# Values' high and low part side by side in one stationary operand, and the meta tokens' small products over 128 rows, in a two-layer hybrid trunk

## The chip, the cores and the metric

The kernel runs on one core of one Trainium2 chip. The metric is the device time of one execution in microseconds. The engines of a core are TensorE (PE in the rows; its weight loads PEld), VectorE (DVE), ScalarE (ACT), GpSimd (POOL) and SyncE (SP), which issues the transfers. TensorE multiplies a stationary operand, up to 128 rows by 128 columns, by a moving one, and adds into PSUM.

## The reference

The input is 512 frames of 1024 features. 16 learned meta tokens stand before them, so 528 positions count; the reference's pads are masked everywhere. There are two layers. Each normalises, multiplies by one wide in-projection, runs two mixers, multiplies each mixer's output by a SiLU gate, and multiplies the whole by an out-projection that is added to the stream.

```python
# layer AB
oa = dsa_attention(...)            # 8 heads of 64: top-k keys by an indexer, softmax, weights @ values
oa = oa.reshape(bsz, P, -1) * jax.nn.silu(ag)
log_a = jax.nn.log_sigmoid((ba @ gate_w2 + gate_b)) / GLA_TAU
ob = gla_chunked(...)              # 4 heads: keys of 64, values of 128, chunks of 64 positions
ob = head_rms(ob).reshape(bsz, P, -1) * jax.nn.silu(bg)
h = h + jnp.concatenate([oa, ob], axis=-1) @ w_out
# layer CD
oc = retention_chunked(...)        # 4 heads like GLA's, with fixed decay
od = stick_breaking(...)           # 8 heads of 64: w = exp(log_sigmoid(z) + after), w @ values
```

What the change touches is the product of a head's weights (queries by keys) with its values, in dsa_attention and stick_breaking, and what is computed for the 16 meta tokens as a chunk of their own in both recurrent mixers.

## The kernel before

Activations lie with features on the partitions and positions in the free dimension. Most products need more digits than TensorE's faster 32-bit type keeps, so operands are split into a high part (`hh`, `wh`, `vh`, `ph`) and a low part, the rest (`hl`, `wl`, `vl`, `pl`). A product of two such numbers is three matmuls: high by high, high by low and low by high. A weight tile `raw` arrives by DMA, ScalarE writes its high part `wh`, VectorE subtracts to get `wl`, and the projections accumulate in PSUM as `acc`.

The four attention pairs of layer AB (A0 to A3) and the four stick-breaking pairs of layer CD (S0 to S3) each treat two heads, the even one and the odd one (`odd`). `pair` (L1070) runs a string of steps: S computes scores and weights for a head, T transposes the weights to have keys on the partitions and splits them into `ph` and `pl` (`weights_turned`, L1039), M does the same for the meta keys (`weights_meta`, L1025, 96 rows that hold high, low and high part), and P (`weighted`, L1057) multiplies by values. The second digit, `u`, is the half of the queries: 256 frames each. The value tiles hold for each pair 192 columns: even head, 64 zeros, odd head (`values`, L966, `value_steps`, L998). `vcols` (L1021) cuts 128 of them, so that the even head's result lands in partitions 0 to 63 and the odd head's in 64 to 127 of one PSUM tile `y` of 512 columns. There is one buffer of y (`pv`). When the pair is done, VectorE multiplies y by the gates into `mx`.

Layer AB begins with the indexer: VectorE finds the top 128 scores of each row by repeated MAX and MATCH_REPLACE on the `lt` tiles. The two pairs of GLA heads (G0, G1) and the values run beside that. The heads of GLA and retention work with 64 rows of keys, and their meta chunk with 16 rows: `gla_steps` (L1331) makes `m`, with the meta keys by queries, their transpose `ktm` (a `mid` buffer), the masked products `attm`, and the products with the meta values `vm` (`head_values`, L1232). `finish_head` (L1392) transposes the 16-row `om`, `residual` (L1405) the 16-row `xm` of each 128-feature part of the input, and `index_weights` (L870) takes 64-row parts of `ba`.

The order of the work is not written out. A recorder keeps every operation (L167), and a planner (`order`, L286) then places them: each engine's next operation is the one that by its costs (`price`, L216) can start first, ties by due time. For TensorE a change of the row class between 32, 64 and 128 costs 95 ns in its plan (`ROWS`), and among operations that are late the ones of the same class are preferred. The program is issued from one line, L406, which is why all rows say L406.

The lines on which most rests:

```python
dst = o[:, P * b0:P * (b0 + nb)]
xh, xl = self.vcols(vh[j], p, odd), self.vcols(vl[j], p, odd)
nc.tensor.matmul(dst, xh, ph, start=False, stop=False)
nc.tensor.matmul(dst, xh, pl, start=False, stop=False)
nc.tensor.matmul(dst, xl, ph, start=False, stop=last and i == len(parts) - 1)
```

Of the kernel before, what the change touches and what calls it, by code (L numbers as in the profile page):

```python
# [9 lines left out]
F32 = mybir.dt.float32  # L10
# [6 lines left out]
P = 128  # L17
# [392 lines left out]
class Kernel:  # L410
# [48 lines left out]
    def vt(self, dt=F32):  # L459
        return self.wk.tile([P, 768], dt, tag="vt", bufs=8, name=self.name("vt"))  # L460
# [228 lines left out]
    def late_consts(self):  # L689
# [8 lines left out]
        self.w2 = self.cp.tile([P, 256], F32, name="w2")  # L698
        nc.sync.dma_start(self.w2[96:112, :], ins["gla_gate_w2"][0])
# [5 lines left out]
        self.attm = [self.cp.tile([NMETA, NMETA], F32, name=f"attm{i}") for i in range(2)]  # L705
        for t in self.attm:
            nc.gpsimd.memset(t, 0.0)
        self.ptm = self.cp.tile([96, 512], F32R, name="ptm")
# [142 lines left out]
    def indexer(self, first, a):  # L851
# [4 lines left out]
        nc.vector.tensor_copy(self.ba[64:128], a[64:128])  # L856
# [13 lines left out]
    def index_weights(self):  # L870
        tr = self.tr()
        for b in range(NB):
            self.transpose(tr[:, 64 * b:64 * b + 64], self.ba[64:128, blk(b)])
        self.nc.vector.tensor_copy(self.iw, tr[:, :256].rearrange("p (b c) -> p b c", b=NB)[:, :, 0:8])
        yield 1
# [90 lines left out]
    def values(self, src, col):  # L966
# [20 lines left out]
        for f in range(4):  # L987
# [7 lines left out]
            self.add(self.value_steps(f, v, vh, vl, vm), self.LAG["v"], f"v{f}")  # L995
        return vh, vl, vm

    def value_steps(self, f, v, vh, vl, vm):  # L998
# [14 lines left out]
        c = slice(P * f, P * (f + 1))  # L1013
        t = self.tr()
        self.transpose(t[:32, :P], z.rearrange("p o c -> p (o c)"))
        self.hi(vm[0:32, c], t[:32, :P])
        self.hi(vm[32:64, c], t[:32, :P])
        self.lo(vm[64:96, c], t[:32, :P], vm[0:32, c])
        yield 1

    def vcols(self, t, p, odd):  # L1021
        return t[:, 192 * p + 64 * odd:192 * p + 64 * odd + P]
# [46 lines left out]

    def pair(self, scores, pm, v, p, gates, tmp, lag, meta=None):  # L1070
# [4 lines left out]
        for word in self.PAIR.split():  # L1075
# [27 lines left out]
        self.nc.vector.tensor_tensor(tmp[:, NMETA:], o, gates[0][:, NMETA:], op=ALU.mult)  # L1103
# [49 lines left out]
    def attention_steps(self, p, qs, ks, kl, strips, gates):  # L1153
# [3 lines left out]
        lm = self.tiny([NMETA, 2, NMETA])  # L1157
# [648 lines left out]
```

## Time and profile before

| what | value |
|---|---|
| runs, median (lowest to highest) | 653.55 us (652.32 to 654.64), 3 runs |
| profiled execution, and its span | 654.6 us, 652.7 us |
| mean granted clock of TensorE | 0.986 of full speed |
| TensorE busy | 633.3 us, 97% of the span |
| VectorE busy | 483.5 us, 74% |
| ScalarE busy | 406.3 us, 62% |
| the chain of waits that ended last | TensorE 78%, VectorE 12%, ScalarE 8% |

The span runs from the first to the last instruction; 1.9 us of the execution lie around it. Names in a row are tiles: `y<-pt,vt` is a matmul that writes y from weights `pt` and values `vt`. A timeline row with a count covers that many instructions that follow each other, and since matmuls overlap, the time that one takes is read from the start of one row to the start of the next. A shape such as 16*128 is the tile of TensorE in use, rows by columns.

### The profile page before, as it was taken

Reading aid. Unit: us, or ns where it says so; the run is one execution under the profiler, and the core shown is the slowest. Engines: PE = TensorE matmul, PEld = TensorE weight load, DVE = VectorE, ACT = ScalarE, POOL = GpSimd, SP = SyncE. Lnnn points to the kernel's source line nnn. Section 1 sums busy time; section 2 is a strip of 40 time slices with the busy share of each in tenths; the row PEclk is TensorE's granted clock in tenths of the full one; section 3 lists DMA queues with packets and bytes.
Section 4 is the critical chain, followed back from the end, with each engine's and each line's share of the span. In section 5 each row is a group of like instructions: output and inputs, shape, how many; then the busy total and the mean of one; then the engine's idle time right before and its main releaser. Section 6 shows DMA issues by size and latency. Waiting matters only on the chain.

```text
span 652.7 us, 12208 instructions
## 1 busy us (share of the span) xinstructions
PE 633.3 (97%) x4469; PEld 582.8 (89%) x4469; DVE 483.5 (74%) x1182; ACT 406.3 (62%) x912; POOL 68.9 (11%) x116
## 2 busy tenths in 40 slices
PE   7999999899999999999999999999999999999995
PEld 6979999898989999999899999888998888988884
DVE  6768799899977859779642674699945699966643
ACT  5656563362344868599643675799844699944434
POOL 4000100120010000001122110001200001110030
PEclk9899999799999999999999999999999999999998
DMA  8437223232322323112243272203322203235403
GB/s 245 111 83 230 66 66 83 58 90 52 80 66 77 89 66 99 50 49 66 65 132 115 65 238 87 66 17 98 82 83 65 77 5 98 65 98 157 150 17 129
DMA packets 91103, 59.25 MB, mean 91 GB/s; under 512 B 7314, under 2 KB 81628, under 8 KB 91044
## 3 DMA queue, kind: packets, MB, share of 16 engines
q1 hardware_dynamic: 91044, 58.48, 31.4%
q8 instruction: 35, 0.57, 0.3%
q14 instruction: 24, 0.20, 0.1%
HBM read 53.18 MB, written 6.90 MB: 92 GB/s over the span
## 4 chain that ended last, share of the span: by engine, by line
PE 78%; DVE 12%; ACT 8%; issue 2%; POOL 0%; DVEq 0%; ACTq 0%; POOLq 0%
PE acc L406 53%; PE x L406 17%; PE y L406 8%; ACT wt L406 4%; DVE st L406 2%; DVE wt L406 2%; DVE wl L406 2%; DVE lt L406 1%; ACT st L406 1%; DVE pt L406 1%; DVE m L406 1%; ACT wh L406 1%; DVE kl L406 1%; ACT ptm L406 1%; ACT pt L406 1%
## 5 line engine op out<-in xcount | busy, mean ns | idle before, releaser
L406 PE MATMUL acc<-hh,wh 128*128 128x272 f32 (+2 forms) x968 | 244.8, 314 | 1.4 <-DVE lt L406 0.4
L406 PE MATMUL acc<-hl,wh 128*128 128x272 f32 (+2 forms) x968 | 236.4, 305 | 0.9 <-DVE hl L406 0.9
L406 PE MATMUL acc<-hh,wl 128*128 128x272 f32 (+2 forms) x968 | 234.6, 303 | 2.1 <-DVE wl L406 2.1
L406 ACT ACTIVATE wh<-raw 128x512 fp32r<-128x512 f32 x154 | 96.1, 631 | 121.5 <-PE acc L406 107.7
L406 PEld LDWEIGHTS acc<-hh,wh 128*128 128x128 f32 x968 | 159.5, 190 | 8.5 <-issue 0.9
L406 PEld LDWEIGHTS acc<-hh,wl 128*128 128x128 f32 x968 | 158.5, 190 | 8.7 <-DVE wl L406 2.9
L406 PEld LDWEIGHTS acc<-hl,wh 128*128 128x128 f32 x968 | 158.6, 190 | 5.4 <-DVE hl L406 1.7
L406 DVE TENSOR_TENSOR wl<-raw,wh 128x512 fp32r<-128x512 f32 x154 | 109.7, 717 | 63.0 <-ACT wh L406 60.7
L406 ACT ACTIVATE wt<-x 128x272 f32<-128x272 f32 (+3 forms) x100 | 43.1, 454 | 24.4 <-PE x L406 15.7
L406 POOL TENSOR_TENSOR gt<-gt,wt 128x528 f32<-128x528 f32 (+1 forms) x16 | 21.7, 1355 | 331.0 <-ACT wt L406 309.7
L406 PE MATMUL x<-st,st 128*128 128x272 f32 (+6 forms) x240 | 50.9, 290 | 0.0
L406 PE MATMUL x<-ident,wt 128*128 128x128 f32 (+2 forms) x300 | 46.0, 274 | 2.0 <-DVE wt L406 1.2
L406 ACT ACTIVATE wt<-wt 128x528 f32<-128x528 f32 (+3 forms) x74 | 43.2, 606 | 3.9 <-DVE wt L406 3.3
L406 PEld LDWEIGHTS x<-st,st 128*128 128x128 f32 (+2 forms) x240 | 37.3, 185 | 7.1 <-ACT wt L406 2.5
L406 ACT ACTIVATE wt<-wt,tiny 128x272 f32<-128x272 f32 (+5 forms) x64 | 34.6, 562 | 9.3 <-DVE tiny L406 8.8
L406 PEld LDWEIGHTS x<-ident,wt 128*128 128x128 f32 (+2 forms) x300 | 34.5, 139 | 6.4 <-DVE pt L406 1.4
L406 PE MATMUL y<-pt,vt 128*128 128x256 f32 (+1 forms) x288 | 39.4, 279 | 0.2 <-DVE pt L406 0.2
L406 PEld LDWEIGHTS y<-pt,vt 128*128 128x128 f32 x288 | 36.6, 190 | 0.9 <-DVE pt L406 0.5
L406 ACT ACTIVATE st<-acc 64x528 fp32r<-64x528 f32 (+1 forms) x58 | 34.7, 599 | 1.0 <-DVE lt L406 0.4
L406 DVE TENSOR_TENSOR_SCAN wt<-wt,wt 128x64 f32<-128x64 f32 (+5 forms) x50 | 30.9, 657 | 2.1 <-ACT wt L406 1.7
L406 ACT ACTIVATE wt<-wt,one 128x528 f32<-128x528 f32 (+3 forms) x42 | 29.5, 704 | 0.2
L406 DVE TENSOR_TENSOR pt<-x,pt 128x384 fp32r<-128x384 f32 (+1 forms) x48 | 28.1, 596 | 1.8 <-ACT pt L406 0.9
(187 smaller groups left out, 884.6 us busy)
## 6 DMA issues: line engine op xcount, KB each, us to landing
raw<-in_w_in_ab_dram SPq DMA_DIRECT2D x64, 256.0 KB, 2.8
raw<-in_w_in_cd_dram SPq DMA_DIRECT2D x56, 256.0 KB, 2.9
raw<-in_w_out_ab_dram SPq DMA_DIRECT2D x16, 256.0 KB, 2.7
raw<-in_w_out_cd_dram SPq DMA_DIRECT2D x16, 256.0 KB, 2.6
rep<-rows SPq DMA_DIRECT2D x8, 328.0 KB, 6.2
lt<-rep SPq DMA_DIRECT2D x8, 264.0 KB, 3.0
pt<-in_x_dram SPq DMA_DIRECT2D x8, 256.0 KB, 4.9
wt<-in_x_dram SPq DMA_DIRECT2D x8, 256.0 KB, 3.1
```

Source lines behind the costliest of these rows:

```text
L406: getattr(getattr(self.core, o.eng), o.name)(*[bind(x) for x in o.args], **{k: bind(x) for k, x in o.kw.items()})
```

## The change

The value tiles become four of 1024 columns: for each pair 256, which hold for the even head its high and then its low part, for the odd head the low and then the high part. The stationary operand of a head is thus [high, low] or [low, high], 128 columns without zeros, and a part is two matmuls, by `ph` and by `pl`. The product of both low parts, left out before, comes with it. y now belongs to one `u`: columns 0 to 255 the even head, 256 to 511 the odd one. Of each head one half of the partitions holds what high values give and the other what low values give. The new `both_parts` adds them: ScalarE copies the other half into a tile `low`, at the head's own partitions, and VectorE adds it to the rest into `tmp`, which the gates then multiply. The meta values `vm` get zero columns, and their product runs once per head.

The small products and transposes named above now run over all 128 rows. The tiles `attm`, `lm`, `ktm`, `vm`, `xm` and `om` are 128 rows high, two of each, and set to zero once by GpSimd; only their first 16 rows are written after that. The 16 zeroing operations of the value tiles go.

```diff
...
-        return self.wk.tile([P, 768], dt, tag="vt", bufs=8, name=self.name("vt"))
+        return self.wk.tile([P, 1024], dt, tag="vt", bufs=4, name=self.name("vt"))
...
         self.w2 = self.cp.tile([P, 256], F32, name="w2")
+        nc.gpsimd.memset(self.w2, 0.0)
...
-        self.attm = [self.cp.tile([NMETA, NMETA], F32, name=f"attm{i}") for i in range(2)]
-        for t in self.attm:
+        few = lambda name, w: [self.cp.tile([P, w], F32, name=f"{name}{i}") for i in range(2)]
+        self.attm, self.lm, self.ktm = few("attm", NMETA), few("lm", 2 * NMETA), few("ktm", P)
+        self.vm, self.xm, self.om = few("vmz", P), few("xm", P), few("om", P)
+        for t in self.attm + self.lm + self.ktm + self.vm + self.xm + self.om:
             nc.gpsimd.memset(t, 0.0)
+        self.nm = self.nom = 0
...
-            self.transpose(tr[:, 64 * b:64 * b + 64], self.ba[64:128, blk(b)])
-        self.nc.vector.tensor_copy(self.iw, tr[:, :256].rearrange("p (b c) -> p b c", b=NB)[:, :, 0:8])
+            self.transpose(tr[:, P * b:P * (b + 1)], self.ba[:, blk(b)])
+        self.nc.vector.tensor_copy(self.iw, tr.rearrange("p (b c) -> p b c", b=NB)[:, :, 64:72])
...
-        vh = [self.vt(F32R) for _ in range(NB)]
-        vl = [self.vt(F32R) for _ in range(NB)]
-        vm = self.wk.tile([96, 512], F32R, tag="vm", bufs=1, name=self.name("vm"))
-        for t in vh + vl:
-            nc.gpsimd.memset(t.rearrange("p (f c) -> p f c", f=4)[:, :, 64:128].bitcast(F32), 0.0)
+        vs = [self.vt(F32R) for _ in range(NB)]
+        vm = self.wk.tile([96, 768], F32R, tag="vm", bufs=1, name=self.name("vm"))
+        nc.gpsimd.memset(vm.rearrange("p (f c) -> p f c", f=4)[:, :, 64:128].bitcast(F32), 0.0)
...
-        heads = lambda x: x[:, 192 * f:192 * f + 192].rearrange("p (o c) -> p o c", c=64)[:, 0:3:2, :]
         for b in range(NB):
             tb = t[:, P * b:P * (b + 1)].rearrange("p (o c) -> p o c", o=2)
-            self.hi(heads(vh[b]), tb)
-            self.lo(heads(vl[b]), tb, heads(vh[b]))
+            x = vs[b][:, 256 * f:256 * (f + 1)].rearrange("p (o c) -> p o c", c=64)
+            self.hi(x[:, 0:4:3, :], tb)
+            self.lo(x[:, 1:3, :], tb, x[:, 0:4:3, :])
...
+    def meta_values(self, vm, p, odd):
+        return vm[:, 192 * p + 64 * odd:192 * p + 64 * odd + P]
...
-    def weighted(self, o, parts, v, p, odd, first, last):
-        nc = self.nc
-        vh, vl, vm = v
-        if first is not None:
-            c = slice(2 * P * first, 2 * P * (first + 1))
-            nc.tensor.matmul(o[:, c], vm[:, P * p:P * (p + 1)], self.ptm[:, c], start=True, stop=False)
+    def weighted(self, o, parts, v, p, odd, u):
+
+
+        nc = self.nc
+        vs, vm = v
+        for h in (0, 1) if odd == 0 else ():
+            nc.tensor.matmul(o[:, 256 * h:256 * (h + 1)], self.meta_values(vm, p, h),
+                             self.ptm[:, 256 * u:256 * (u + 1)], start=h == 0, stop=False, skip_group_check=True)
         for i, (j, b0, nb, ph, pl) in enumerate(parts):
-            dst = o[:, P * b0:P * (b0 + nb)]
-            xh, xl = self.vcols(vh[j], p, odd), self.vcols(vl[j], p, odd)
-            nc.tensor.matmul(dst, xh, ph, start=False, stop=False)
-            nc.tensor.matmul(dst, xh, pl, start=False, stop=False)
-            nc.tensor.matmul(dst, xl, ph, start=False, stop=last and i == len(parts) - 1)
+            at = 256 * odd + P * (b0 - 2 * u)
+            x = vs[j][:, 256 * p + P * odd:256 * p + P * (odd + 1)]
+            for k, w in enumerate((ph, pl)):
+                nc.tensor.matmul(o[:, at:at + P * nb], x, w, start=False, stop=k == 1 and i == len(parts) - 1,
+                                 skip_group_check=True)
+
+    def both_parts(self, o, tmp, u):
+        nc = self.nc
+        c = slice(NMETA + 256 * u, NMETA + 256 * (u + 1))
+        t = self.wk.tile([P, 256], F32, tag="low", bufs=2, name=self.name("low"))
+        for h in range(2):
+            r, q = slice(64 * h, 64 * h + 64), slice(64 - 64 * h, 128 - 64 * h)
+            nc.scalar.copy(t[r], o[q, 256 * h:256 * (h + 1)])
+        for h in range(2):
+            r = slice(64 * h, 64 * h + 64)
+            nc.vector.tensor_tensor(tmp[r, c], o[r, 256 * h:256 * (h + 1)], t[r], op=ALU.add)
...
-                if o is None:
+                if odd == 0:
                     o = self.pv()
-                self.weighted(o, turned.pop((odd, u)), v, p, odd, u if odd == 0 else None, odd == 1)
+                self.weighted(o, turned.pop((odd, u)), v, p, odd, u)
+                if odd:
+                    self.both_parts(o, tmp, u)
...
-        self.nc.vector.tensor_tensor(tmp[:, NMETA:], o, gates[0][:, NMETA:], op=ALU.mult)
+        self.nc.vector.tensor_tensor(tmp[:, NMETA:], tmp[:, NMETA:], gates[0][:, NMETA:], op=ALU.mult)
...
-                nc.tensor.matmul(t[:, :NMETA], v[2][:, P * p:P * (p + 1)], mm[0], start=True, stop=True)
+                for h in range(2):
+                    nc.tensor.matmul(t[:, :NMETA], self.meta_values(v[1], p, h), mm[0], start=h == 0, stop=h == 1)
...
-            nc.tensor.matmul(a[:, c], self.w2[96:112, P * p:P * (p + 1)], self.ba[96:112, c], start=True, stop=True)
+            nc.tensor.matmul(a[:, c], self.w2[:, P * p:P * (p + 1)], self.ba[:, c], start=True, stop=True)
...
-        nc.tensor.matmul(m[:NMETA, 0:16], ks[0:64, :NMETA], qs[0:64, :NMETA], start=True, stop=True)
-        nc.vector.copy_predicated(attm, self.tri[:NMETA, :NMETA], m[:NMETA, 0:16])
-        self.transpose(m[:NMETA, 32:96], kh[0:64, :NMETA])
-        ktm = self.mid([NMETA, 64])
-        nc.vector.tensor_copy(ktm, m[:NMETA, 32:96])
+        nc.tensor.matmul(m[:NMETA, 0:16], ks[:, :NMETA], qs[:, :NMETA], start=True, stop=True)
+        nc.vector.copy_predicated(attm[:NMETA], self.tri[:NMETA, :NMETA], m[:NMETA, 0:16])
+        self.transpose(m[:NMETA, 384:512], kh[:, :NMETA])
+        ktm = self.ktm[head % 2][:, :64]
+        nc.vector.tensor_copy(ktm[:NMETA], m[:NMETA, 384:448])
...
-        xm = self.mid([NMETA, P])
+        xm = self.xm[f % 2]
...
-        self.transpose(t[:, :NMETA], xm)
+        self.transpose(t[:, :P], xm)
...
```

On TensorE, the last P step of the second stick pair, S1, its even head's first matmuls; `pt_74` and `pt_75` are `ph` and `pl`, `vt_10` and `vt_11` high parts of two key blocks, `vt_14` and `vt_15` low parts, and in the changed program `vt_6` to `vt_9` hold both. Before:

```order
L406 MATMUL y_12_6297<-ptm_106,vm_3_5373 128x256
L406 MATMUL y_12_6297<-pt_74_6390,vt_10_4521 128x256
L406 MATMUL y_12_6297<-pt_75_6410,vt_10_4521 128x256
L406 MATMUL y_12_6297<-pt_74_6390,vt_14_4542 128x256
L406 MATMUL y_12_6297<-pt_74_6390,vt_11_4525 128x256
L406 MATMUL y_12_6297<-pt_75_6410,vt_11_4525 128x256
L406 MATMUL y_12_6297<-pt_74_6390,vt_15_4548 128x256
```

Now:

```order
L406 MATMUL y_18_6456<-ptm_116,vm_3_4538 128x256 x2
L406 MATMUL y_18_6456<-pt_74_6414,vt_6_5343 128x256
L406 MATMUL y_18_6456<-pt_75_6421,vt_6_5343 128x256
L406 MATMUL y_18_6456<-pt_74_6414,vt_7_5359 128x256
L406 MATMUL y_18_6456<-pt_75_6421,vt_7_5359 128x256
L406 MATMUL y_18_6456<-pt_76_6423,vt_8_5368 128x256
L406 MATMUL y_18_6456<-pt_77_6427,vt_8_5368 128x256
```

Where three matmuls stood for a part there are two, and the meta matmul stands twice at the head of the step.

On VectorE, the top-k search while the first GLA head runs; `lt` are index scores, `m8` eight largest values, `x_66` is that head's `m`. Before:

```order
L406 MAX m8_22_1675<-lt_4_635 128x8
L406 TENSOR_TENSOR wl_32_1682<-raw_32_1465,wh_32_1669 128x512
L406 MAX m8_23_1691<-lt_5_646 128x8
L406 MAX m8_24_1699<-lt_6_690 128x8
L406 COPY_PREDICATED attm0_104<-tri_99,x_66_1697 16x16
L406 MATCH_REPLACE lt_5_646<-m8_23_1691,lt_5_646 128x400
L406 MATCH_REPLACE lt_6_690<-m8_24_1699,lt_6_690 128x528
L406 COPY mid_3_1718<-x_66_1697 16x64
```

Now:

```order
L406 COPY_PREDICATED attm0_104<-tri_99,x_66_1682 16x16
L406 MAX m8_22_1687<-lt_4_644 128x8
L406 TENSOR_TENSOR wl_32_1694<-raw_32_1477,wh_32_1680 128x512
L406 COPY ktm0_108<-x_66_1682 16x64
L406 MAX m8_23_1708<-lt_5_655 128x8
L406 MAX m8_24_1715<-lt_6_699 128x8
L406 MATCH_REPLACE lt_5_655<-m8_23_1708,lt_5_655 128x400
```

The writing of `attm0` has moved in front of three MAX operations and a weight's low part, and the copy to `ktm0` too.

On ScalarE, the first stick pair, S0, up to the cast of weight tile 103; `wt` are scores and weights of queries by keys, `y_15` is the first y of the stage. Before:

```order
L406 ACTIVATE wt_172_5886<-x_218_5881 128x256
L406 ACTIVATE wt_164_5778<-wt_164_5778 128x400
L406 ACTIVATE wt_172_5886<-wt_172_5886 128x528
L406 ACTIVATE wt_174_5923<-x_217_5870 128x272
L406 ACTIVATE wt_172_5886<-wt_172_5886,one_82 128x528
L406 ACTIVATE wt_174_5923<-x_218_5881 128x256
L406 ACTIVATE wh_103_5938<-raw_103_5609 128x512
```

Now:

```order
L406 ACTIVATE wt_168_5863<-wt_168_5863 128x528
L406 ACTIVATE wt_170_5901<-x_217_5849 128x272
L406 ACTIVATE wt_168_5863<-wt_168_5863,one_82 128x528
L406 ACTIVATE wt_170_5901<-x_218_5868 128x256
L406 ACTIVATE wt_160_5761<-wt_160_5761 128x400
L406 COPY low_10_5919<-y_15_5854 64x256 x2
L406 ACTIVATE wh_103_5925<-raw_103_5592 128x512
```

The two copies of `low_10` and one more operation on a weight tile stand between the scores' copies and `wh_103`.

## Rows read from the trace of the kernel before

**Rows 1.** The page, first lines: span, then busy us (share) xinstructions

```profile
span 652.7 us, 12208 instructions
...
PE 633.3 (97%) x4469; PEld 582.8 (89%) x4469; DVE 483.5 (74%) x1182; ACT 406.3 (62%) x912; POOL 68.9 (11%) x116
```

**Rows 2.** Busy by stage: stretch, length, engines (xinstructions), PEclk, DMA share, GB/s

```profile
80.00:184.00 104.00, 99.05 (x759) 93.32 (x758) 100.17 (x287) 44.49 (x98) 10.29 (x18) 0.97 0.28 70
220.00:320.00 100.00, 98.75 (x805) 96.62 (x804) 79.28 (x274) 81.89 (x193) 5.85 (x8) 1.00 0.23 65
416.00:471.00 55.00, 53.83 (x360) 48.00 (x359) 50.78 (x108) 53.38 (x118) 5.15 (x4) 1.00 0.22 60
517.00:572.00 55.00, 53.81 (x362) 48.23 (x361) 50.85 (x107) 53.06 (x118) 5.84 (x5) 1.00 0.22 62
```

**Rows 3.** Waits of PE: who waits for whom: us in total, times, longest us

```profile
PE x L406 <- DVE attm L406: 1.7, 1, 1.7
```

**Rows 4.** Busy time by stretch, behind that wait

```profile
119.50:126.50 7.00, 7.00 (x31) 6.02 (x32) 6.12 (x18) 1.40 (x4) 0.13 (x1) 0.51 0.24 62
```

**Rows 5.** Timeline of PE, 470.5 to 475.5: start us, us, instruction, xcount

```profile
471.34 0.28 PE L406 MATMUL y<-ptm,vm 96*128 96x256 f32 x1
471.46 2.93 PE L406 MATMUL y<-pt,vt 128*128 128x256 f32 x24
474.22 0.45 PE L406 MATMUL acc<-hh,wh 128*128 128x512 f32 x1
```

**Rows 6.** The page, costliest groups: xcount, busy us, mean ns, idle before

```profile
L406 PE MATMUL y<-pt,vt 128*128 128x256 f32 (+1 forms) x288 | 39.4, 279 | 0.2 <-DVE pt L406 0.2
```

**Rows 7.** Groups of ACT and DVE by form: xcount, busy us, mean ns, idle

```profile
L406 ACT ACTIVATE wt<-x 128x256 f32<-128x256 f32 x24 | 9.7, 404 | 4.0 <-PE x L406 3.9
...
L406 DVE SCALAR_TENSOR_TENSOR st<-acc,wt 64x256 f32<-64x256 f32 x16 | 6.7, 420 | 0.2
```

**Rows 8.** Timeline of PE, 333.9 to 337.5

```profile
333.79 0.41 PE L406 MATMUL acc<-hl,wh 128*128 128x272 f32 x2
334.03 0.41 PE L406 MATMUL acc<-hh,wl 128*128 128x272 f32 x2
334.37 0.23 PE L406 MATMUL x<-ident,mid 16*128 16x16 f32 x1
334.53 0.66 PE L406 MATMUL x<-ident,wt 128*128 128x128 f32 x4
334.94 0.48 PE L406 MATMUL acc<-hh,wh 128*128 128x272 f32 x2
```

**Rows 9.** Groups of PE by form, 16-row transposes to 16 columns

```profile
L406 PE MATMUL x<-ident,mid 16*128 16x16 f32 x8 | 1.8, 230 | 0.0
```

**Rows 10.** Timeline of PE, 144.2 to 146.2

```profile
144.64 0.40 PE L406 MATMUL acc<-hh,wl 128*128 128x272 f32 x2
144.97 0.43 PE L406 MATMUL x<-vm,mid 16*64 16x128 f32 x2
145.32 0.39 PE L406 MATMUL x<-vm,attm 16*16 16x128 f32 x2
145.64 0.82 PE L406 MATMUL x<-gv,wt 128*128 128x128 f32 x5
```

**Rows 11.** Timeline of PE, 485.6 to 487.5

```profile
485.65 0.38 PE L406 MATMUL y<-gv,wt 128*128 128x128 f32 x2
...
487.36 0.37 PE L406 MATMUL acc<-hh,wh 128*128 128x272 f32 x1
```

**Rows 12.** Timeline of PE, 437.5 to 438.5

```profile
437.58 0.50 PE L406 MATMUL acc<-hh,wl 128*128 128x512 f32 x1 [1.02 <-DVE wl L406]
437.93 0.39 PE L406 MATMUL acc<-hh,wh 128*128 128x512 f32 x1
438.16 0.27 PE L406 MATMUL x<-ident,pm 128*32 128x128 f32 x1
438.27 0.49 PE L406 MATMUL x<-ident,wt 128*128 128x128 f32 x3
```

More of the change, by code (lines that the diff above doesn't have):

```diff
@@ L855, in indexer @@
         self.ba = self.lt()
-        nc.vector.tensor_copy(self.ba[64:128], a[64:128])
+        nc.vector.tensor_copy(self.ba, a)
         ik, ikl = self.st(F32R), self.st(F32R)
@@ L994, in values, with value_steps @@
             nc.scalar.copy(v, a)
-            self.add(self.value_steps(f, v, vh, vl, vm), self.LAG["v"], f"v{f}")
-        return vh, vl, vm
-    def value_steps(self, f, v, vh, vl, vm):
+            self.add(self.value_steps(f, v, vs, vm), self.LAG["v"], f"v{f}")
+        return vs, vm
+    def value_steps(self, f, v, vs, vm):
         nc = self.nc
@@ L1006, in value_steps @@
             self.transpose(t[:, P * b:P * (b + 1)], v[:, blk(b)])
-        heads = lambda x: x[:, 192 * f:192 * f + 192].rearrange("p (o c) -> p o c", c=64)[:, 0:3:2, :]
         for b in range(NB):
             tb = t[:, P * b:P * (b + 1)].rearrange("p (o c) -> p o c", o=2)
-            self.hi(heads(vh[b]), tb)
-            self.lo(heads(vl[b]), tb, heads(vh[b]))
+            x = vs[b][:, 256 * f:256 * (f + 1)].rearrange("p (o c) -> p o c", c=64)
+            self.hi(x[:, 0:4:3, :], tb)
+            self.lo(x[:, 1:3, :], tb, x[:, 0:4:3, :])
         yield 1
-        c = slice(P * f, P * (f + 1))
+        c = lambda r: vm[r, 192 * f:192 * (f + 1)].rearrange("p (o c) -> p o c", c=64)[:, 0:3:2, :]
         t = self.tr()
         self.transpose(t[:32, :P], z.rearrange("p o c -> p (o c)"))
-        self.hi(vm[0:32, c], t[:32, :P])
-        self.hi(vm[32:64, c], t[:32, :P])
-        self.lo(vm[64:96, c], t[:32, :P], vm[0:32, c])
+        tv = t[:32, :P].rearrange("p (o c) -> p o c", o=2)
+        self.hi(c(slice(0, 32)), tv)
+        self.hi(c(slice(32, 64)), tv)
+        self.lo(c(slice(64, 96)), tv, c(slice(0, 32)))
         yield 1
-    def vcols(self, t, p, odd):
-        return t[:, 192 * p + 64 * odd:192 * p + 64 * odd + P]
+    def meta_values(self, vm, p, odd):
+        return vm[:, 192 * p + 64 * odd:192 * p + 64 * odd + P]
     def weights_meta(self, pm, g):
@@ L1156, in attention_steps @@
         tmp = self.mx[:, p]
-        lm = self.tiny([NMETA, 2, NMETA])
+        lm, lmz = [x(self.lm[p % 2]) for x in (lambda t: t[:NMETA].rearrange("p (o c) -> p o c", o=2), lambda t: t)]
         pm = self.pmt()
@@ L1214, in meta @@
                 t = self.tr()
-                self.transpose(t[:32, :NMETA], lm.rearrange("p o c -> p (o c)"))
+                self.transpose(t[:32, :P], lmz)
                 pmm = self.sm.tile([96, NMETA], F32R, tag="pmm", bufs=2, name=self.name("pmm"))
@@ L1239, in head_values @@
         self.transpose(t[:NMETA, :P], v[:, :NMETA])
-        vm = self.sm.tile([NMETA, P], F32, tag="vm", bufs=2, name=self.name("vm"))
-        self.nc.scalar.copy(vm, t[:NMETA, :P])
+        vm = self.vm[self.nm % 2]
+        self.nm += 1
+        self.nc.scalar.copy(vm[:NMETA], t[:NMETA, :P])
         return vt, vm
@@ L1253, in heads, with head_norm @@
             gates.append(self.gate(w, cg + P * head, frames=frames))
-    def head_norm(self, src, n, center):
+    def head_norm(self, src, n, center, out=None):
         nc = self.nc
@@ L1259, in head_norm @@
         bc = lambda x: x[:n, :c].unsqueeze(2).broadcast_to([n, c, P])
-        out = self.wt()
+        out = self.wt() if out is None else out
         ov = out[:n, :c * P].rearrange("p (c e) -> p c e", c=c)
@@ L1361, in gla_steps @@
         nc.vector.tensor_copy(ss[0:64, 0:P], m[:64, 128:256])
-        om = self.head_norm(m[:NMETA, 256:384].unsqueeze(1), NMETA, False)
+        om = self.head_norm(m[:NMETA, 256:384].unsqueeze(1), NMETA, False, self.om[head % 2])
         yield 1
@@ L1400, in finish_head @@
             t = self.tr()
-            self.transpose(t[:, :NMETA], om[:NMETA, :P])
+            self.transpose(t[:, :P], om)
             nc.vector.tensor_tensor(tmp[:, :NMETA], t[:, :NMETA], gate[:, :NMETA], op=ALU.mult)
@@ L1408, in residual @@
         xt = self.wt()
-        xm = self.mid([NMETA, P])
+        xm = self.xm[f % 2]
         nc.sync.dma_start(xt[:, :512].rearrange("p (b c) -> p b c", b=NB),
                           ins["x"][0, :, P * f:P * (f + 1)].rearrange("(b p) c -> p b c", p=P))
-        nc.sync.dma_start(xm, ins["meta_tokens"][:, P * f:P * (f + 1)])
+        nc.sync.dma_start(xm[:NMETA], ins["meta_tokens"][:, P * f:P * (f + 1)])
         yield 6
@@ L1534, in retention @@
                                 self.xi[:, p:p + 1, :].broadcast_to([P, NB, P]), op=ALU.mult)
-        kz, kzm = self.wt(), self.mid([NMETA, P])
+        kz, kzm = self.wt(), self.ktm[p]
         turned = []
@@ L1552, in key_steps @@
         for h in range(2):
-            nc.scalar.activation(kzm[:, 64 * h:64 * h + 64], t[:NMETA, 64 * h:64 * h + 64], AF.Copy,
+            nc.scalar.activation(kzm[:NMETA, 64 * h:64 * h + 64], t[:NMETA, 64 * h:64 * h + 64], AF.Copy,
                                  scale=self.zeta[:NMETA, 1, 2 * p + h:2 * p + h + 1])
```

## The prediction

> **What bounds the kernel now.** I read the page's first lines, then the busy times by stage, the waits of TensorE, and single stretches of its timeline. TensorE is busy 633.3 of the span's 652.7 us, VectorE 483.5, ScalarE 406.3 [rows 1]. So TensorE sets the time almost everywhere, and its idle time is only 19.4 us. By stage the margins differ [rows 2]. From 80 to 184 us, where the top-k search runs, VectorE is busy 100.17 of 104.00 us, so it is the second bound there. In the attention stage (220 to 320) VectorE has 20.7 us to spare and ScalarE 18.1. In the two stick-breaking stages (416 to 471, 517 to 572) ScalarE is busy 53.38 and 53.06 of 55 us: 1.6 and 1.9 us to spare, and VectorE 4.2. The longest single wait in mid-run is 1.7 us for VectorE's `attm` [rows 3], and behind it, from 119.50, the granted clock is 0.51 for 7.00 us [rows 4]. At half clock that stretch does what 7.00 x 0.51 = 3.6 us do at full, so it costs 3.4 us on top of the wait.
>
> The sum is made against the profiled execution: 654.6 us, of which the span is 652.7. The median of the runs is 653.55, 1.05 less, so I take 1.05 off at the end.
>
> **Part A: values' two parts side by side.** In a P step of a pair the meta matmul and 24 matmuls of weights by values run together. The last one of the second stick pair starts its 24 at 471.46, and the next projection starts at 474.22: 2.76/24 = 0.115 us each; the meta one before takes 471.34 to 471.46 = 0.12 [rows 5]. The program has 288 such matmuls in eight pairs [rows 6], three to a part. Two to a part are 192. So 96 x 0.115 = 11.0 us go. Added: the meta matmul runs once per head, 16 more, 16 x 0.12 = 1.9 us; the meta queries' own product twice in four pairs, 4 matmuls of 16 columns, 0.1 us. Net on TensorE -9.0 us, 1.1 per pair.
>
> The other half of each head's sum now lies in the wrong partitions of PSUM, so each of 16 y tiles is followed by two ScalarE copies and two VectorE additions of 64 x 256. The trace has no such copy. The nearest rows are ScalarE's 128 x 256 read from PSUM, 404 ns, and VectorE's 64 x 256 operation with one PSUM input, 420 ns [rows 7]. As duration hardly depends on partitions, I take these: 32 x 0.404 = 12.9 us on ScalarE, 32 x 0.420 = 13.4 on VectorE. The totals become 419 and 497 us, below TensorE's. The product with the gates reads SBUF in place of PSUM and moves nowhere; I cost it at nothing. y has one buffer, so the next y tile waits until these four are done, 2 x 0.404 + 2 x 0.420 = 1.65 us after the last matmul. What hides it is TensorE's other work: between the last use of one y tile and the first of the next the new order has 55 rows or more of other matmuls in the stick pairs, and 33 to 120 in the attention pairs; 33 rows of 0.11 us are 3.6 us, enough unless ScalarE has 2 us of other work ahead of the copies. If that cover were gone in all, 16 x 1.65 = 26.4 us would be lost.
>
> **Part B: small products over 128 rows.** A change between 16-, 32- or 64-row and 128-row matmuls costs time on both sides. At 334 us two projections take 0.24 (333.79 to 334.03), but the two before the 16-row transpose take 0.34 (334.03 to 334.37); the transpose holds 0.16, to 334.53; a 128-row one is (334.94 - 334.53)/4 = 0.10 [rows 8]. So one such transpose costs 0.10 + 0.06 too much, 0.15 with a margin, and there are eight of the residual's, one for each of its 128-column parts [rows 9], 1.2 us. In a GLA head the entry costs 0.09 (two projections take 144.64 to 144.97 = 0.33 in place of 0.24) and the four passes of `vm` by `mid` and `attm` last from 144.97 to 145.64 = 0.67 [rows 10]; four 128-row passes cost 4 x 0.107 = 0.43, from 16 passes in 1.71 us [rows 11]. That saves 0.33 per head, 1.3 in four. Of the program's 84 changes of row class between neighbouring matmuls 20 are left. The 64 that go are 16 with the residual's transposes, 8 with the GLA heads, and 40 others; at 0.09 each (rows 8 and 10 give 0.08 to 0.10), 3.6 us. Part B: 1.2 + 1.3 + 3.6 = 6.1 us.
>
> The Trainium skill ("TensorEngine Tiling (Array Packing)", Key Properties) says that switching the tiling mode drains TensorE, and by its wording a change in columns alone is one too. Here a 512-column projection before a 32-column transpose is followed after 0.23 us (437.93 to 438.16), as much as 512 x 0.12/272 by the undisturbed 272-column ones of rows 8, and the transpose holds 0.11 [rows 12]. So the trace does not bear out a price for columns. By the page's rule all mode changes would count, of which only 30 of 178 go in place of 64 of 84, and the gain would be about 3 us smaller, an estimate.
>
> The zeroing of the padded tiles is POOL's, which is busy 68.9 us in all [rows 1], and it replaces 16 memsets of the old value tiles. It runs while the first weights come in; I cost it at nothing, and at most 1 us if the first projection were to wait for it.
>
> **What is lost on the way.** TensorE -15.1 us counts in full only where nothing else ends last.
> - Top-k stage: about 2.6 us of part B lie there (three GLA heads, 1.0, and 18 changes, 1.6). VectorE has 3.8 us of idle in 104 [rows 2], and works off a list in the same order. I take half, 1.3 lost; bounds 0 and 2.6. In VectorE's new order the `attm` step of the first head stands four operations earlier, some 2.3 us, and TensorE reaches it as much earlier, so the 1.7 us wait and its clock stretch should stay; bounds: both stay, or both go (-5.1).
> - Attention stage: 16 copies, 6.5 us, in 18.1 idle. A few will be in the way of an Exp: 0.6.
> - Each stick stage: eight copies, of which two come behind its end since the last P step is there [rows 5]. Six are 6 x 0.404 = 2.4 us against 1.6 and 1.9 of idle, and the weights' cast `wh_103` stands behind two of them and one more Exp, so its low part and the projections on it come 1.3 us later. Fewer matmuls also make TensorE ask sooner. I take 1.0 us lost in each, 2.0 in all; bounds 0 and 3.2 each (all eight on the path).
> - The order elsewhere is a new list. The two costliest waits with what follows them are the 5.1 us above; an equal one could appear. I take nothing.
>
> Loss 1.3 + 0.6 + 2.0 = 3.9. So 654.6 - 15.1 + 3.9 = 643.4, on the median's footing 642.3 us.
>
> **Rivals.**
> 1. All of it is kept: 654.6 - 15.1 = 639.5, or 638.4 as a median; with the `attm` wait and the slow clock gone too, 633.3. For it: TensorE is 97% busy [rows 1]. Against it: the second bounds of rows 2.
> 2. In the stick stages ScalarE becomes the bound and TensorE's waits get long enough that its clock falls, as it did behind the `attm` wait. Two stretches like that of rows 4 cost 2 x 3.4 = 6.8, with 0.8 of waits: 643.4 + 7.6 - 1.05 = 650, between 646 with one and 652.5. For it: 1.6 us of idle; TensorE already waits 1.02 us at 437.58 for `wl` [rows 12]. Against it: that wait was followed by no slow stretch, since both stages show a clock of 1.00 [rows 2].
> 3. Slower: ScalarE is the bound in all eight pairs. Then part A's TensorE time is worth nothing and the copies are added: 654.6 - (6.1 - 1.3) + 12.9 = 662.7, 661.6 as a median. It decides from the point where ScalarE has no idle left through the pairs. For it: the stick stages. Against it: 18.1 us of idle in the attention stage.
> 4. No change: gains in A are hidden by ScalarE in the stick stages and by a lost order elsewhere, 653.5.
>
> The Trainium skill (the same page, PSUM Bottleneck) warns that a faster TensorE does not speed up the emptying of PSUM, and that the copy may then bound. ScalarE's 53.38 of 55 us [rows 2] agrees with that for the stick stages, its 81.89 of 100 does not for attention.
>
> **How the numbers follow.** The forecast, 642.3 with a range of its own from 639.5 to 646: 0.50. Rival 1: 0.18. Rival 2: 0.21. Rival 3: 0.07. Rival 4: 0.04. About 0.3%, 2 us, is what a measurement of this kernel can tell from none, so faster is below 651.6 and slower above 655.5. Of rival 2, 0.02 lies within. Faster 0.50 + 0.18 + 0.19 = 0.87, same 0.02 + 0.04 = 0.06, slower 0.07. The range is 634.5 to 651: it leaves out rivals 3 and 4, the far end of rival 2 and part of 633.3, under 0.2.
>
> **What would show it.** In the profile after: 192 matmuls of weights by values at some 0.115 us; TensorE's busy time down by about 15 us if clock stretches stay; `low` copies near 0.4 us, 32 of them, and 32 additions. Between neighbouring projections and the residual's transposes no 0.10 us gap is left. In the stick stages ScalarE's idle is next to nothing, and TensorE's idle there is 1 to 2 us more than before. The forecast is wrong if TensorE waits for `wh`, `wl` or y for more than 2 us in a stick stage, if a new stretch with half the clock appears or the one at 119.50 goes, or if y's single buffer shows as a wait for `low` or the additions.

## The result, and the profile after

The changed kernel takes 649.33 us (median of 8 runs, 647.76 to 651.65) where the one before takes 653.96 in the same runs: a ratio of 0.9934, interval 0.9916 to 0.9951. It is faster by 4.6 us, where 11.3 were forecast. The profiled executions are 654.6 and 647.8 us. Times go with the mean granted clock: where a run's clock is on record, the kernel before takes 652.1 to 652.8 us at 0.991 to 0.992 and 652.8 to 654.6 at 0.985 to 0.987, of which its profile is one; the changed one 647.8 at 0.993, which is its profile, and 651.65 at 0.981. So the two profiles differ by 6.8 us, the medians by 4.6.

The page after answers to [rows 1]:

```profile
span 646.0 us, 12128 instructions
...
PE 619.8 (96%) x4393; PEld 570.0 (88%) x4393; DVE 494.3 (77%) x1214; ACT 417.0 (65%) x944; POOL 67.8 (10%) x113
```

TensorE is busy 13.5 us less, but its idle time has grown from 19.4 to 26.2 us. ScalarE and VectorE have 10.7 and 10.8 us more. The stages answer to [rows 2], shifted with their work:

```profile
79.10:180.00 100.90, 95.36 (x764) 91.10 (x764) 95.69 (x277) 44.38 (x98) 10.71 (x18) 1.00 0.29 73
215.20:314.00 98.80, 96.03 (x771) 92.71 (x769) 83.98 (x284) 86.33 (x208) 6.25 (x8) 1.00 0.23 63
409.60:464.60 55.00, 52.25 (x341) 45.70 (x340) 50.01 (x108) 54.16 (x120) 5.18 (x4) 1.00 0.19 53
510.50:565.50 55.00, 52.27 (x342) 45.83 (x341) 49.98 (x108) 53.77 (x120) 4.66 (x4) 1.00 0.19 53
```

In the stick stages TensorE now is idle 2.75 us of 55 where it was 1.17, and ScalarE is the fullest engine there. In attention TensorE's idle share grew from 1.2 to 2.8%, though ScalarE has 12 us to spare. The stretch behind the `attm` wait, which is still 1.55 us long, answers to [rows 4]:

```profile
115.00:126.00 11.00, 9.85 (x80) 9.33 (x81) 10.62 (x31) 3.72 (x9) 2.28 (x2) 1.00 0.21 50
```

Its clock is 1.00 in this execution, so the stretch at half clock is absent, behind a wait of nearly the same length. If it is the same stretch that parts the executions of the kernel before (argued: only one was traced), it is worth 1.7 us by their medians, 654.2 and 652.5, and not 3.4. By the stages below it is less: the run with the parts only has the old small products and no such stretch in its top-k stage, which takes 142.0 us against 143.0.

Three groups, of TensorE's products by values and of the new operations of ScalarE and VectorE (count, busy us, mean ns):

```profile
L406 PE MATMUL y<-pt,vt 128*128 128x256 f32 x192 | 28.9, 279 | 0.3
```

```profile
L406 ACT COPY low<-y 64x256 f32<-64x256 f32 x32 | 11.7, 367 | 7.2 <-PE y L406 6.7
```

```profile
L406 DVE TENSOR_TENSOR mx<-y,low 64x256 f32<-64x256 f32 x32 | 13.4, 419 | 3.3 <-PE acc L406 1.8 <-ACT low L406 1.1
```

The copies cost 0.367 us and the additions 0.419 (0.404 and 0.420 were taken). Ahead of the copies ScalarE also stands idle for 6.7 us in all until y is there, which the forecast left out. From start to start the products of weights and values took 34.0 us before and take 22.7 now (-11.3), the meta matmuls +1.9 and the meta queries' own +0.5: -8.9 for part A, against -9.0. TensorE's busy time as a whole is 5.9 us below that of the run with padding only (625.7), at the same clock; where the other 3 us are was not traced.

Part B at its two places, the GLA head of [rows 10] and the residual of [rows 8], TensorE's timeline (start us, length, count):

```profile
139.44 0.40 PE L406 MATMUL acc<-hh,wl 128*128 128x272 f32 x2
139.77 0.43 PE L406 MATMUL x<-vmz,ktm 128*64 128x128 f32 x2
140.13 0.39 PE L406 MATMUL x<-vmz,attm 128*16 128x128 f32 x2
140.45 0.52 PE L406 MATMUL acc<-hh,wh 128*128 128x272 f32 x2
```

```profile
327.36 0.60 PE L406 MATMUL x<-ident,wt 128*128 128x128 f32 x4
327.80 0.27 PE L406 MATMUL x<-ident,xm 128*128 128x128 f32 x1
327.82 0.49 PE L406 MATMUL acc<-hh,wh 128*128 128x272 f32 x2
```

The residual's transposes behave as foretold: five in 0.46 us, 327.36 to 327.82, and no gap. In this GLA head nothing was gained, and the four passes take 0.68 in the other three too. The two projections ahead still take 0.33 us and the four passes 139.77 to 140.45 = 0.68, as against 0.67 before. The rows are 128 now, but the tile is 64 and 16 columns wide, and that change costs as much.

Now a stick stage. TensorE's waits in it, then the chain that ended last, each step with its length:

```profile
PE x L406 <- DVE pm L406: 2.1, 2, 1.2
PE acc L406 <- DVE wl L406: 0.4, 1, 0.4
```

```profile
410.87 0.62 ACT wh L406
...
415.82 3.32 ACT wt L406 x8
...
422.92 4.27 ACT wt L406 x10
...
427.21 0.37 ACT low L406
...
427.59 0.36 ACT low L406
...
427.98 0.63 ACT wh L406
...
442.34 2.85 ACT wt L406 x6
...
445.22 0.37 ACT low L406
...
446.97 0.37 ACT low L406
...
449.78 0.43 DVE mx L406
...
455.28 0.60 DVE mx L406
455.88 6.02 DVE wt L406 x6
...
462.52 1.05 PE x L406 x8
```

From 410.87 to 448.59 the chain runs on ScalarE without a break, with the `low` copies in it, then on VectorE, with additions (`mx`, 0.43 us) and a product with the gates (`mx`, 0.60), until `pm` is there at 462.48 and TensorE goes on. Before, TensorE took the chain over at 437.58 and kept it to the end of the stage:

```profile
433.01 2.21 DVE wt L406 x3
...
436.85 0.09 DVE pm L406
...
437.58 0.73 PE acc L406 x2
...
439.30 1.63 PE acc L406 x7
...
453.92 2.92 PE acc L406 x24
...
467.08 1.34 PE acc L406 x11
```

To compare whole stages I take the start of the 48th, 312th, 552nd, 720th and 960th of the 968 `acc<-hh,wh` matmuls, which all kernels have (us between them in the profiled execution; differences in the text are of unrounded times). The last column has the starts of the stretches in these stages in which TensorE's granted clock was half, the lower of its two levels:

| kernel | top-k stage | attention | layer border | stick stages | half clock from |
|---|---|---|---|---|---|
| before | 143.0 | 142.4 | 76.7 | 180.1 | 119.6 |
| changed | 139.7 | 141.7 | 75.1 | 180.0 | none |
| padding only | 139.8 | 141.4 | 75.1 | 179.8 | none |
| parts only | 142.0 | 144.3 | 76.7 | 180.6 | 324.3 |
| parts in stick pairs | 139.8 | 141.3 | 75.1 | 179.9 | none |
| parts in attention pairs | 139.7 | 141.6 | 75.1 | 179.8 | none |
| no copies | 141.1 | 140.9 | 75.1 | 177.4 | 117.4 |
| third matmul back | 139.8 | 148.2 | 74.9 | 182.5 | 326.8 |
| copies twice | 141.1 | 149.3 | 74.6 | 182.2 | 117.2, 318.6, 328.9 |
| no sum | 141.0 | 144.3 | 75.2 | 182.1 | 116.5, 304.2, 437.3, 539.7 |
| one copy | 139.7 | 142.2 | 75.1 | 178.8 | 319.8 |
| one copy, stick pairs only | 139.8 | 141.3 | 75.1 | 176.9 | none |
| all pairs but A3 | 139.8 | 143.0 | 75.2 | 176.9 | none |

The stretch of the kernel before lasts 7 us, each of the others 3.4 us, in which 1.7 us of work at full clock are lost (3.4 x 0.50, an estimate). The 9 us of TensorE that part A saved are in no column: with both halves of the change, attention takes 141.7 us and the stick stages 180.0, with padding alone 141.4 and 179.8. What the changed kernel's profile is shorter than that of padding alone, 1.7 us, lies ahead of these stages, where no weights meet values: its 48th matmul starts at 46.6 us, that one's at 48.9.

### The profile page after: what moved, and what is told of

It reads as the page before. It is cut to its first block, busy times and chain, and to the rows that moved or that the text cites. A ratio compares the mean times of both kernels' runs of the same rounds, so it can differ in the third digit from the quotient of the medians.

```text
span 646.0 us, 12128 instructions
## 1 busy us (share of the span) xinstructions
PE 619.8 (96%) x4393; PEld 570.0 (88%) x4393; DVE 494.3 (77%) x1214; ACT 417.0 (65%) x944; POOL 67.8 (10%) x113
## 4 chain that ended last, share of the span: by engine, by line
PE 62%; ACT 18%; DVE 16%; issue 3%; POOL 0%; DVEq 0%; ACTq 0%; POOLq 0%
PE acc L406 43%; PE x L406 14%; ACT wt L406 10%; PE y L406 5%; DVE wt L406 4%; ACT st L406 3%; DVE wl L406 2%; DVE st L406 2%; ACT wh L406 2%; ACT pt L406 1%; DVE lt L406 1%; DVE pt L406 1%; DVE mx L406 1%; DVE m L406 1%; DVE kl L406 1%
## 5 line engine op out<-in xcount | busy, mean ns | idle before, releaser
L406 DVE TENSOR_TENSOR wl<-raw,wh 128x512 fp32r<-128x512 f32 x154 | 108.1, 706 | 50.6 <-ACT wh L406 49.3
L406 PE MATMUL x<-ident,wt 128*128 128x128 f32 (+1 forms) x296 | 44.9, 276 | 2.6 <-DVE wt L406 1.2
L406 ACT ACTIVATE wt<-wt 128x400 f32<-128x400 f32 (+3 forms) x74 | 43.3, 602 | 3.9 <-DVE wt L406 3.1
L406 PEld LDWEIGHTS x<-ident,wt 128*128 128x128 f32 (+1 forms) x296 | 33.4, 139 | 7.1 <-DVE wt L406 1.4
L406 PE MATMUL y<-pt,vt 128*128 128x256 f32 x192 | 28.9, 279 | 0.3
L406 PEld LDWEIGHTS y<-pt,vt 128*128 128x128 f32 x192 | 25.5, 189 | 2.0 <-DVE pt L406 1.8
```

The source lines that it names most:

```text
L406: getattr(getattr(self.core, o.eng), o.name)(*[bind(x) for x in o.args], **{k: bind(x) for k, x in o.kw.items()})
```

## The experiments

Each was run in five rounds; a ratio is to the kernel before on the same chip.

**One half of the change at a time.** The first keeps the old value tiles and three matmuls, the second the old small products.

```diff
-        vs = [self.vt(F32R) for _ in range(NB)]       # padding only: vh, vl as before
-        self.transpose(t[:, :P], xm)                  # parts only: 16 rows as before
```

> Theory: the pair stages and the top-k stage of the changed kernel are held by ScalarE and VectorE, so TensorE time saved there buys nothing. Padding alone then gains the residual's eight transposes (1.2 to 1.5 us) and the start (0.8), and loses the rest in the top-k stage, where VectorE is the bound: 651 to 652.5 us against 654.0 for the kernel before; 3.5 less if the slow-clock stretch behind the attm wait goes too. Rival, the sum of the prediction: the padding's 6.1 us of TensorE are kept, 648 us.

Padding alone: 649.22 us, 0.9934 [0.9918, 0.9949], the whole gain of the change by the medians, in the top-k stage (3.1 us, with the missing slow stretch) and at the layer border. The time alone does not part theory and rival, since its clock is 0.993 in most runs; the stages do: 1.6 us are gained at the layer border, 1.0 in attention, 0.4 in the stick stages. What padding is worth in the top-k stage without any slow stretch shows between parts only and the changed kernel: 142.0 and 139.7, 2.3 us of the 2.6 that the prediction counted there.

> Only the values' two parts side by side, with its copies and additions, no padding. Theory: the four stick pairs gain nothing (their 4.6 us of TensorE lie beside ScalarE and VectorE), the attention pairs 1 to 2.5 of 4.6: 651.5 to 653.5 us against 654.0. Rival, the prediction's sum: about 9 less 2.6 of waits, 647.5. Second rival, the copies are the bound in all pairs: 660 or more.

Parts alone: 659.02, 1.0082 [1.0062, 1.0101], slower than before by 5.4 by the ratio. Its runs lie at clocks from 0.981 to 0.990; the profiled one, 656.4, is the fastest, so most of the loss lies in executions that were not traced. In the traced one attention is 1.9 us longer; TensorE waits 1.21 us there for `pt`, and from 323 to 329 the mean clock is 0.72. The half clock begins at 324.3, some 7 us behind that wait and behind shorter ones (0.37 and 0.57 us). Theory and first rival missed this loss; the second rival's 660 is near, but the stick stages are only 0.4 us longer than before, so the copies do not bind in all pairs. Why the same parts lose nothing beside the padding is not settled.

```profile
317.55 0.99 PE L406 MATMUL x<-ident,wt 128*128 128x128 f32 x7 [1.21 <-DVE pt L406]
```

```profile
323.00:329.00 6.00, 5.16 (x27) 4.31 (x26) 3.56 (x7) 3.65 (x9) 0.31 (x1) 0.72 0.36 106
```

**Copies out, copies twice, TensorE's work back.**

```diff
-            nc.scalar.copy(t[r], o[q, 256 * h:256 * (h + 1)])
+            nc.vector.tensor_tensor(tmp[r, c], o[r, ...], self.none[r], op=ALU.add)   # zeros
...
+            for _ in range(2): nc.scalar.copy(...)                   # copies twice
...
+            for k, w in enumerate((ph, ph, pl)):                     # third matmul back
```

> The changed kernel without the 32 ScalarE copies: each VectorE addition adds a tile of zeros in place of the low half, so the low values' part is left out of the sum. VectorE's work stays. Theory: ScalarE's chain in the stick stages is 1.5 us shorter each and TensorE and VectorE become the bound there, 1.5 to 2.3 us less in each, and 1 to 2 in attention: 643.5 to 646 us against 649.3 for the changed kernel. Rival, the new list of instructions costs the time and not the copies: 648.5 to 650.

645.54, 0.9880 [0.9862, 0.9898]: the theory's time. The stick stages give 2.7 us for 5.9 us of copies, attention 0.7 for as many.

> The changed kernel with each of the 32 ScalarE copies run twice into the same tile, 11.7 us more on ScalarE and nothing on TensorE. Leaving them out gave 3.8 us. Theory: the pairs' chain runs over ScalarE, so a second set costs as much or more, 3.8 to 6: 653 to 655.5 us. Rival, the copies lie in ScalarE's idle time and the run without them gained from its other list of instructions: 649 to 650.5 us.

659.16, 1.0096 [1.0082, 1.0110]: 9.8 us for 11.7 us of copies, more than expected. The stick stages pay 2.2; attention pays 7.6, of which some 3.4 are two slow stretches that lie behind waits (here TensorE's clock is the third number from the end):

```profile
318.00:323.00 5.00, 4.96 (x28) 4.72 (x29) 2.97 (x8) 2.18 (x6) 0.00 (x0) 0.66 0.17 49
328.00:333.00 5.00, 4.71 (x26) 4.71 (x27) 2.65 (x5) 2.56 (x6) 0.00 (x0) 0.66 0.15 44
```

> The changed kernel with the third matmul of each part put back (the product with the high part of the weights runs twice and counts double): 96 matmuls, 11.0 us of TensorE, and nothing less on ScalarE or VectorE. Theory: in the stick stages they lie beside ScalarE's and VectorE's chain and cost 0 to 1 us each, in attention 2 to 4: 651.5 to 655 us against 649.3. Rival, TensorE is still the bound in the pairs: 649.3 + 11 = 660.

657.12, 1.0066 [1.0048, 1.0083]: 7.8 us for 11.0 us of matmuls, between theory and rival. The stick stages pay 2.5 for 5.5, about as much as for 5.9 us of copies. So both engines lie on the chain by turns there, and what the change took from one it gave to the other. Attention pays 6.6 for 5.5, of which some 1.7 is a slow stretch.

**The sum left out.** Gates multiply y directly.

```diff
+            nc.vector.tensor_tensor(tmp[r, c], o[r, ...], gates[0][r, c], op=ALU.mult)
```

> No copies and no additions: per head and half the gates multiply y from PSUM (32 VectorE operations of 64 x 256), the low values' part is left out of the result. Against the kernel without copies VectorE has 5.5 us less. Theory: with no extra work on either engine the pairs are TensorE's again and most of its 9 us are kept: 642 to 645 us. Rival, the pairs' time is set by the new list or by waits between the engines that were there before: 645 to 649.

653.53, 1.0016 [1.0005, 1.0028]: theory and rival both fall short. With less work on both engines TensorE waits 2.3 us for `pm` in each stick stage, and the clock falls behind it:

```profile
PE x L406 <- DVE pm L406: 2.3, 1, 2.3
```

```profile
436.00:442.00 6.00, 5.54 (x26) 4.08 (x25) 4.86 (x9) 5.92 (x13) 0.00 (x0) 0.72 0.15 44
```

Four stretches at half clock lie in this execution, three more than in that without copies: some 5.1 (an estimate, 3 x 1.7) of the 7.3 us between their spans, 651.8 and 644.5. Nor is less work the only difference: each half of a pair now needs its gates before y is read, not the whole pair at its end. In the first stick stage the gates are ready at 434.23 and y is read at 435.58, where the changed kernel reads it at 430.52 and has the gates at 440.51. So this run shows what such a wait can cost through the clock; whether a shorter engine gains anything by itself it does not show.

**By stage.** The parts in the stick pairs or in the attention pairs alone, padding everywhere.

```diff
+    NEW = {"w_in_ab": False, "w_in_cd": True}
```

> The padding everywhere, and values' two parts side by side in the stick pairs alone; attention as before. Theory: in the stick stages 2.3 us of TensorE go and 2.9 of ScalarE come, both on a chain that runs partly over each, so the net is nothing: 648.5 to 650 us, as with padding alone (649.2). Rival, the prediction's sum for these stages (2.3 less 1.0, twice): 646.6.

> The padding everywhere, and values' two parts side by side in the attention pairs alone; stick pairs as before. Theory: through three pairs 1 to 2 us are gained, and at the end of the last one, where no projections are left to fill in, ScalarE's and VectorE's longer way to the out-projection gives it back, with a stretch of slow clock in some runs: 648 to 651 us. Rival, the prediction's sum for this stage (4.6 less 0.6): 645.2.

649.85 (0.9950 [0.9936, 0.9965]) and 648.84 (0.9942 [0.9921, 0.9962]). Both are what the theory said: neither gives anything measurable on top of the padding. (`low` has one buffer in these two, in the changed kernel two.) In the second the 480th matmul comes 0.9 us sooner after the 312th (90.2 against 91.2 with padding alone), and the 552nd 1.2 later after the 480th (51.4 against 50.2): gained in attention and given back at its end.

**A cheaper sum.** Both heads with the high part first, so one copy does.

```diff
-            self.lo(x[:, 1:3, :], tb, x[:, 0:4:3, :])
+            self.lo(x[:, 1:4:2, :], tb, x[:, 0:4:2, :])
...
+        nc.scalar.copy(t, o[64:128])
```

> Both heads with their high part first, so that both low halves of y lie in the upper 64 partitions and one ScalarE copy of 64 x 512 does for two of 64 x 256. About 0.58 for 2 x 0.367 us, 16 times: 2.4 us less on ScalarE. Theory, at the 0.33 us that a us of copies was worth when they were left out: 648 to 649 us against 649.3. Rival, what counts is the number of operations between the last matmul and the sum: 647.

> The stick pairs alone with parts side by side, and one copy of 64 x 512 in place of two (the low half goes to one of the general work tiles). Theory: 1.2 us less ScalarE time in each stick stage than with two copies, worth 0.5 each: 648 to 649 us. Rival, no copy matters: same as the stick pairs with two copies.

All pairs: 647.29, 0.9920 [0.9906, 0.9933], the rival's 647; the copy takes 0.583 us. Stick pairs alone: 646.26, 0.9899 [0.9884, 0.9914], below the theory's 648, the fastest complete version, 3.0 us under padding alone. There TensorE has the chain again, from 432.77 to the end of the stage:

```profile
424.21 4.27 ACT wt L406 x10
...
432.07 0.65 ACT wt L406
...
432.77 0.76 PE x L406 x5
...
437.06 2.31 PE y L406 x18
...
449.47 2.94 PE acc L406 x24
...
457.25 3.08 PE acc L406 x25
```

The gain over two copies, 3.6 us, is more than the 8 x (0.734 - 0.583) = 1.2 us taken from ScalarE in the four pairs (the expectation counted them double). The low half also has another tile with more buffers, and the stages part the two: one copy into `low` takes the stick stages from 180.0 to 178.8, one copy into a work tile to 176.9, here and in the run with all pairs but A3 below. In these two the second copy of a stage starts 11.7 us after the first, with `low` 17.8 (428.13 and 445.97): another order of the work. They are as short as the stages without any copies (177.4), so a copy's price hangs on where it stands in the chain, not on its 0.583 us alone.

> As the one-copy kernel, and the product with the gates, whose operands are both in SBUF now, runs on GpSimd in place of VectorE: 8 x 0.69 = 5.5 us off VectorE, GpSimd's operation takes about 1.3 us. Theory (VectorE is on the chain in the pairs): 1 to 2 us less than one copy alone, 646 to 648 us; if the longer product at the end of attention is what the out-projection waits for, 0.6 later there. Rival, VectorE has idle time enough: same as one copy.

650.60, 0.9968 [0.9957, 0.9980], 3.3 us slower than one copy with VectorE's product, so theory and rival both fall. GpSimd's product takes 1.62 us, not 1.3; attention is 3.5 longer, with a wait of 2.0 us for `hl` and two stretches at half clock where one copy has one. The reservation decided, at more than its price.

**Controls.** Another list of the same work (`MARGIN = 250`), the meta products over 128 columns, and all pairs but A3.

> The changed kernel with one number of the planner changed (a margin of 250 in place of 300 ns in TensorE's choice), no operation added or left out: what another list of the same work is worth. Theory: within 1.5 us of 649.3. Rival, the lists decide: 3 us or more apart, and then the differences between the other kernels can't be put down to their loads.

648.62, 0.9941 [0.9922, 0.9959], 0.7 from the changed kernel: this one other list moves less than the differences of 2 us and more used above; those below 1 us it does not bear out.

> Padding only, and in GLA's heads the meta products of vm by ktm and by attm have 128 columns too. In the changed kernel their four passes still take 0.68 us and the two projections before them 0.33, as with 16 rows. Theory: what is left there is a change of column class (64 and 16 columns), which costs as much as one of rows; with 128 columns the four passes take 0.43 and the entry nothing, 0.3 us a head, of which VectorE's stage keeps most: 648.3 to 649.2 against 649.2 for padding alone. Rival, the time is that of the products' own shape and stays 0.68.

648.49, 0.9929 [0.9914, 0.9945]. It is padding only with these columns, against 649.22. The entry is 0.24 for two projections and the four passes 0.36, as the theory said:

```profile
141.06 0.41 PE L406 MATMUL acc<-hh,wl 128*128 128x272 f32 x2
141.30 0.38 PE L406 MATMUL x<-vmz,ktm 128*128 128x128 f32 x2
141.52 0.39 PE L406 MATMUL x<-vmz,attm 128*128 128x128 f32 x2
141.66 0.49 PE L406 MATMUL acc<-hh,wh 128*128 128x272 f32 x2
```

> Padding, one copy of 512 columns, and the parts side by side in all pairs but the last attention pair, A3, which keeps three matmuls and no copies. Theory: up to the end of attention some 1 us is gained as in the one-copy kernel, and the stretch to the residual, 50.2 us with padding alone, 51.3 with the change and 52.3 with one copy in all pairs, is 50.2 to 50.5 again, since the loss sits in the last pair, where no projections are left: 644.5 to 646 us, the fastest so far (646.3 with the stick pairs alone). Rival, the loss sits in all attention pairs or in chance waits: 647 or more.

647.46, 0.9914 [0.9898, 0.9931]. The theory falls: the end of attention is no shorter (52.1 us from the 480th matmul to the 552nd, 52.3 with one copy in all pairs), with TensorE waiting 1.5 us for `hl` and 1.1 for `gt`. The loss does not sit in the last pair alone. What holds attention as a whole, beyond the copies, is open; in the kernel without copies the chain from 286 to 305 us still runs mostly over VectorE (`hl`, `wt`, `pt`).

## Why the prediction was wrong

- **Part A on TensorE** (-9.0): right by its rows, -8.9; of it the meta queries' product is +0.5, not +0.1. The prices of copies and additions were right within 0.04 us.
- **"Loss 1.3 + 0.6 + 2.0 = 3.9"** is the step that failed, in its terms for the pairs. Part A was to give 9.0 - 0.6 - 2.0 = 6.4 us and gave nothing: 649.22 us with padding alone, 649.33 with both halves. Its 4.6 us in the stick stages were lost whole, not 2.0 of them, and so were its 4.5 in attention, not 0.6. I set the new copies against ScalarE's idle time, as if idle time anywhere in a stage could take them. In the stick stages the copies lie on a chain of dependent work, in which the engines take turns: the runs with copies or matmuls added or taken out show either priced at about 0.4 us a us there, 2.7 us back without the copies and 2.5 lost with the matmuls. In attention, where most of the miss lies, leaving the copies out gave back only 0.7 of the 4.5, though matmuls put back cost 6.6 there. So TensorE's time does count in attention, and other work must have cost what it saved, the additions or the new order; which of them stays open.
- The Trainium skill ("TensorEngine Tiling (Array Packing)", PSUM Bottleneck) warns that copies out of PSUM may become the bound when TensorE gets faster. The stick stages agree, with ScalarE busy 54.16 of 55 us; attention does not show it, at 86.33 of 98.80.
- **Part B** (-6.1, less 1.3 in the top-k stage): padding alone gained 3.9 us, with the slow stretch in it, of 4.8. Of the top-k stage's 2.6 some 2.3 came, so 1.3 was too much to take off there. The residual's 1.2 came (1.6 at the layer border). The 1.3 of the GLA heads did not show at their products: what failed there is the reading of [rows 12], that columns cost nothing. It was taken from a 32-column transpose and used for 64- and 16-column products; the run with 128 columns shows 0.36 in place of 0.68 us. The Trainium skill (the same page, Key Properties) says that changing the tiling mode drains TensorE. These products agree, 0.33 in place of 0.24 us for the two projections ahead; the 32-column transpose of [rows 12] does not show it. The 3.6 us of the 40 other changes were not measured by themselves.
- **The slow stretch** was priced at 3.4 us from its length. By stages it was worth 1.0, by the medians 1.7.
- **Rivals.** Rival 2 came closest in time, 650, by luck: ScalarE became the bound in the stick stages, but the two slow stretches that make up most of its price are not in the traced execution. The mechanism that came is in rival 3 and in the first half of rival 4: part A's TensorE time is worth nothing. The copies were not added on top, as rival 3 had it.
- **Signs.** The cover of y held: no matmul into y waits for `low` or the additions. The `attm` wait stayed, as forecast, but its slow stretch is gone from the traced execution, one of the signs named for a wrong forecast. The longest wait in a stick stage is 1.2 us, for `pm`, which was not among those named.

## What to carry to other kernels

Before counting an engine's saving, read which engines hold the chain of waits in that stage: where the chain passes between engines, work moved from one to the other cancels at its share of the chain, whatever the idle times say. Look for the sum's cheapest form at once: with both low halves on one side a single copy took the stick stages from 180.0 to 178.8 us, and a tile with more buffers for it to 176.9. A price read from one shape of tile is good for that shape. And compare profiles at the same granted clock: here the two differ by 6.8 us, the medians by 4.6.

## What the runs showed of the hardware

- A change to a tile of 64 or 16 columns costs 0.09 us at entry and keeps four passes at 0.68 us; at 128 columns they take 0.36 (one of four heads 0.47). A 32-column transpose between projections cost nothing: 0.23 us from the 512-column projection ahead to it and 0.11 for itself [rows 12].
- A wait of 1.55 us was followed by full clock, one of 1.68 in the same place by half clock for 7 us. In the run without the sum a wait of 2.28 us that ended at 435.72 was followed by half clock from 437.3; in the run with parts only a wait of 1.21 that ended at 317.55 was followed by full clock until 324.3.
- ScalarE copies 64 x 256 from PSUM into other partitions in 0.367 us and 64 x 512 in 0.583; VectorE adds 64 x 256 of PSUM and SBUF in 0.419. GpSimd's product of 128 x 512 takes 1.62 us, VectorE's 0.68.
